# Conformer, attention and experts in one kernel: the normalisation after the convolution by blocks, six taps moved to TensorE

## The chip, the cores and the metric

One core of one Trainium2 chip runs the whole model block. The metric is the device time of one execution in microseconds (us). Before the change it is 1229.51 us, the median of three runs (1229.46 to 1229.88).

## What is computed

The input x is 256 tokens by 1024 channels in float32. Layer 0 is a Conformer convolution module and a dense SwiGLU; layer 1 is attention with forget gates (16 heads) and a SwiGLU of 8 experts of which each token takes 2; an RMSNorm stands before each part and at the end. The change touches the Conformer module alone:

```python
def conformer_conv(h, w_in, b_in, w_dw, b_dw, ln_g, ln_b, w_out, b_out):
    u = h @ w_in + b_in                       # 1024 -> 2048
    a, gate = jnp.split(u, 2, axis=-1)
    u = a * jax.nn.sigmoid(gate)
    u = depthwise_conv(u, w_dw) + b_dw        # 31 taps back in time, each channel by itself
    u = layer_norm(u, ln_g, ln_b)             # over the 1024 channels of a token
    u = jax.nn.silu(u)
    return u @ w_out + b_out
```

## The kernel before, in words

Channels lie in 8 tiles of 128 partitions; the 256 tokens are two blocks of 128, which here are called block 0 and block 1. A float32 matrix product is made of three products of high and low parts (`mm3`): every weight tile of 128x1024 is copied by ScalarE to a high part `wh`, and VectorE subtracts it from the weight to give the low part `wl` (`split`, L93 to L95). One such pair is what the text calls a split. `emit_split` issues the next one; five may stand ready. Weight tiles of 1 MB come by DMA into a ring of 10 slots; when a tile has been used up, `drop` gives its slot to the next tile in a fixed order, and SyncE issues the load, in order, when the slot's last reader is done. `later` is a list of pieces of work that are issued one by one at each use of a weight part, so that other engines' work is put between products.

Every engine does its instructions in the order in which the program issues them. That order is written by hand. In the Conformer module it is:

1. `glu_mm`, `glu_tr`: the products with w_in, the gate (a Sigmoid on ScalarE, L563) and transposes, so that channels lie in partitions.
2. The convolution, by channel tile. Tiles 2, 3, 6 and 7 are products with diagonal weights on TensorE (`conv_pe`, 64 records of 128 columns each). Tiles 0 and 4 are 31 multiply-adds each on VectorE (`conv_dve`). Tile 1 and the first 25 taps of tile 5 are a multiplication on ScalarE into one of four buffers `pr` and an addition on GpSimd each (`conv_pool`, L639 and L640). The last `SHARE` = 6 taps of tile 5 are made on VectorE into `p5` (`shared`, L701), and L720 adds the two parts of tile 5. A list `steps`, sorted by a time written for each step (L711 to L719), sets how these are mixed; the first four splits of w_out stand in it at 17, 20, 23 and 26.
3. The mean over channels: `mean(o)`, a product of each channel tile with a matrix of 1/1024, summed over the 8 tiles in `pm`. Tiles 0 to 3 are issued between the convolution's products, tiles 4, 6, 5 and 7 after the last of them (L722).
4. The variance (L732 to L752): a copy of the mean (`mu`), subtraction of the mean from four halves (VectorE three, GpSimd one), squares on ScalarE, sums over partitions by products with a column `onesd`. The first half's four tiles go to TensorE as they are; the other three halves are first summed over tiles by VectorE (L745). Both blocks' sums lie in one `pq`. A Silu on `mu` makes ScalarE load the table of Silu.
5. `rsqrt` for both blocks at once: small instructions on VectorE, one after another. Then `lrs` is spread over the partitions by a product with the identity into `pb`, and VectorE scales c (`scale_c`, L762), ScalarE applies Silu with gain and bias (L770), VectorE makes high and low parts (L773, L774), block 0 ahead of block 1.
6. The products with w_out (`colmm`, L787): for each half of the columns, block 0 (24 products and one of the bias), then block 1.

`warm(n)` issues n products of 128x128 ones on TensorE whose result nobody reads. Each float32 product shows as two records in the trace. From the dense SwiGLU on, the program is the same before and after.

Of the kernel before, what the change touches and what calls it, by code (L numbers as in the profile page):

```python
# [35 lines left out]
LAG = 2  # L36
SILU = 2
REP = 8
WARM = [16, 9, 2, 8, 8, 7, 8, 5]
HOLD = 2  # L40
SPLITH = 2
WPOOL = 2
# [1 line left out]
DVE_RATE = 0.65  # L44
POOL_RATE = 0.8
SHARE = 6
WHOLE = (5, 15, 25)
PAD = 15
SEG = PAD + P
# [5 lines left out]
def tile_trunk(ctx: ExitStack, tc: tile.TileContext, a):  # L55
# [17 lines left out]
    def mm(o, l, r, start, stop):  # L73
        pe.matmul(o, l, r, start=start, stop=stop)  # L74
# [15 lines left out]
    def f32(t):  # L90
        return t.bitcast(F32)
# [61 lines left out]
    def add(fill, gain=None, width=512, subs=2):  # L153

        tiles.append((fill, gain, width, subs))
        i = len(tiles) - 1
        first[i] = len(order)
        order.extend((i, j) for j in range(subs))
        return i

    def load(t, src):
        src = src() if callable(src) else src
        m = 2 if st["load"] == 0 else 1
        for k in range(m):
            c = slice(k * SLOT // m, (k + 1) * SLOT // m)
            nc.sync.dma_start(t[:, c], src[:, c])
# [5 lines left out]
    def cols(w, gain=None, n=512):  # L172

        m = SLOT // n
        return [add(lambda t, x=next(w): load(t, x), gain and (gain, k), n, 2) for k in range(0, DO, m)][0]
# [32 lines left out]
        free.append(slot_of.pop(i))  # L208
        push()

    def emit_split():
        n = st["split"]
        i, j = order[n]
        _, gain, width, subs = tiles[i]
        src = slot_of[i][:, 1024 * j:1024 * j + 1024]
        if gain == "whole":
            parts[n] = (src,)
            st["split"] += 1
            return
        hi = cst.tile([P, 1024], F32R, name="wh", tag="wh", bufs=NSPLIT)  # L220
        lo = cst.tile([P, 1024], F32R, name="wl", tag="wl", bufs=NSPLIT)
        if gain is None:
            split(hi, lo, src, g if st.get("pool") and n % st["pool"] == 0 else v)
        else:
            for q in range(1024 // width):
                k = gain[1] + j * (1024 // width) + q
                c = slice(q * width, q * width + width)
                x = gain[0][:, k:k + 1]
                s.activation(hi[:, c], src[:, c], AF.Copy, scale=x)  # L229
                v.scalar_tensor_tensor(lo[:, c], src[:, c], x, f32(hi[:, c]), ALU.mult, ALU.subtract)  # L230
        parts[n] = (hi, lo)
        st["split"] += 1
        if j == subs - 1:
            drop(i)

    def split_ahead():
# [35 lines left out]
    w = stream(a["dense"])  # L272
    L_in = [cols(w) for _ in range(4)]
    L_diag = [add(lambda t, x=next(w): load(t, x), subs=0) for _ in range(8)]
    L_wout = [cols(w) for _ in range(2)]
    L_ffn = add_ffn(w, vcol("ffn", 0))
    gk = vcol("kv")
# [15 lines left out]
    L_moe = [add_moe(i, WHOLE if i % 2 else ()) for i in range(E)]  # L293


    def rsqrt(dst, var, mul=1.0, add=0.0):

        n = var.shape[-1]
        hv, y, q = (tmp.tile([P, 2], F32, name=x, tag=x, bufs=1)[:, :n] for x in ("hv", "y", "q"))
        sh = tmp.tile([P, 2], I32, name="sh", tag="sh", bufs=1)[:, :n]  # L300
        v.tensor_scalar(hv, var, 0.5 * mul, 0.5 * add, ALU.mult, ALU.add)
        v.tensor_scalar(sh, hv.bitcast(I32), 1, None, ALU.arith_shift_right)
        v.tensor_scalar(y.bitcast(I32), sh, -1.0, float(0x5F3759DF - 2 ** 22 - 2 ** 31), ALU.mult, ALU.add)
        for it in range(3):
            for b in range(n):
                c = slice(b, b + 1)
                v.scalar_tensor_tensor(q[:, c], y[:, c], hv[:, c], y[:, c], ALU.mult, ALU.mult)
            v.scalar_tensor_tensor(dst if it == 2 else y, q, 1.5, y, ALU.subtract, ALU.mult)

    def sum_squares():  # L310
        ms = tmp.tile([P, 2], F32, name="ms", tag="ms", bufs=1)
# [159 lines left out]
    with convs:  # L471
# [57 lines left out]
        warm(WARM[5])  # L529
        lay(0)  # L530
        lay(1)

# [158 lines left out]
        p5 = phases(bank("dn")[:, :NT])  # L691

        def mean(o):
            mm(pm, onesq, cT[:, o], o == 0, o == DO - 1)

        def shared(j):
            w = wdwT[:, 5, j:j + 1]
            if j == CW - SHARE:
# [6 lines left out]
        def at_time(t, dt, fs):  # L705
            for f in fs:
                steps.append((t, len(steps), f))
                t += dt
            return t

        t = at_time(1.5, 0.42, qd + taps_of(conv_dve, 4))  # L711
        at_time(t, 0.42, [lambda j=j: shared(j) for j in range(CW - SHARE, CW)])
        at_time(1.5, 0.8, qp + taps_of(conv_pool, 5)[:CW - SHARE])
        at_time(7.8, 0, [out2])
        at_time(14.8, 0, [out3] + [lambda o=o: mean(o) for o in range(4)])
        at_time(21.8, 0, [out6])
        at_time(17, 3, [emit_split] * 4)
        for _, _, f in sorted(steps):
            f()  # L719
        v.tensor_tensor(c5, c5, p5, ALU.add)  # L720
        conv_pe(7)()
        for o in (4, 6, 5, 7):  # L722
            mean(o)
        warm(WARM[1])


# [2 lines left out]
        sq = [xp[:, t].rearrange("p (o c) -> p o c", c=P) for t in range(2)]  # L729
        halves = (slice(0, 4), slice(4, 8))  # L730
        mu = cv.tile([P, 2, HP], F32, name="mu")
        s.activation(mu, pmb[1], AF.Copy)  # L732
        pq = bank("dn")
        for t in range(2):
            for x in halves:
                c = cb[t][:, x]
                on_pool = t == 1 and x is halves[0]
                (g if on_pool else v).tensor_tensor(
                    c, c, (mu if on_pool else pmb[t])[:, None].to_broadcast([P, 4, 2, HP]), ALU.subtract)
                s.activation(sq[t][:, x].rearrange("p o (b m) -> p o b m", b=2), c, AF.Square)  # L740
        for o in range(4):
            mm(pq[:, 0:1], sq[0][:, o], onesd, o == 0, False)
        for t, x in ((0, halves[1]), (1, halves[0]), (1, halves[1])):
            sr = cv.tile([P, P], F32, name="sr", tag="sr", bufs=2)
            v.tensor_reduce(sr, sq[t][:, x].rearrange("p o c -> p c o"), AX.X, ALU.add)  # L745
            warm(WARM[2])
            mm(pq[:, t:t + 1], sr, onesd, False, t == 1 and x is halves[1])
        s.activation(mu, mu, AF.Silu)
        lrs = cv.tile([P, 2], F32, name="lrs")
        lv = cv.tile([P, 2], F32, name="lv")  # L750
        v.tensor_scalar(lv, pq[:, :2], EPS, None, ALU.add)
        rsqrt(lrs, lv)  # L752
        warm(WARM[3])
        pb = bank("dn")
        for t in range(2):
            mm(pb[:, P * t:P * t + P], lrs[:, t:t + 1].to_broadcast([P, P]), ident, t == 0, t == 1)

        warm(WARM[4])

        def scale_c(t, x):  # L760
            r = pb[:, P * t:P * t + P].rearrange("p (b m) -> p b m", b=2)[:, None]
            v.tensor_tensor(cb[t][:, x], cb[t][:, x], r.to_broadcast([P, x.stop - x.start, 2, HP]), ALU.mult)  # L762

        scale_c(0, slice(0, 2))
        scale_c(0, slice(2, 8))
        for t in range(2):
            h, l = [y[:, :, P * t:P * t + P].rearrange("p o (m b) -> p o b m", b=2) for y in hT]
            for o in range(DO):
                c = cb[t][:, o]
                s.activation(c, c, AF.Silu, scale=vcol("lng")[:, o:o + 1], bias=vcol("lnb")[:, o:o + 1])  # L770
                if o % 2 or t == 0 and o == 0:
                    x = slice(o - 1 if o > 1 or t else o, o + 1)
                    v.tensor_copy(h[:, x], cb[t][:, x])  # L773
                    v.tensor_tensor(l[:, x], cb[t][:, x], f32(h[:, x]), ALU.subtract)  # L774
                if t == 0 and o in (3, 5):
                    scale_c(1, halves[o // 2 - 1])

        for hf in range(2):
            ps = [bank() for _ in range(2)]
# [20 lines left out]
    with tc.tile_pool(name="att", bufs=1, reuse_waits="tile") as ap:  # L800
# [272 lines left out]
        rms_inv(R2)  # L1073
        logit(1, 0)
        logit(1, 1)
        warm(WARM[6])
        high(0, 1)
        high(1, 0)
        lg = ap.tile([P, 2, E], F32, name="lg")
# [14 lines left out]
        warm(WARM[7])  # L1094
# [310 lines left out]
def _laid_out(i):  # L1405
# [26 lines left out]
    for q in range(8):  # L1432

        ch = P * (4 * (q // 4) + 2 + q % 4 // 2) + HP * (q % 2) + c
        for b in range(2):
            diag[q, HP * b + c, 1 - b:32 - b, c] = dw[:, ch].T
    w_in, w_out, kvf, wq = i["conv_w_in"][0], i["conv_w_out"][0], i["w_kvf"], i["w_q"][0]
    dense = [cols(w_in, c0) for c0 in (0, 1024, 512, 1536)] + [diag.reshape(8, P, SLOT)]
# [55 lines left out]
```

## Time and profile before

| | |
|---|---|
| time, median of 3 runs | 1229.51 us (1229.46 to 1229.88) |
| profiled execution, its own time | 1228.05 us |
| its span, first to last instruction | 1226.3 us |
| mean granted clock of TensorE | 0.992 |
| busy share: PE, DVE, ACT, POOL | 96%, 80%, 70%, 8% |
| DMA | 356.17 MB, mean 290 GB/s |

PE is TensorE's matrix products, PEld its weight loads, DVE VectorE, ACT ScalarE, POOL GpSimd, SP SyncE. Times in the rows are in us from the start of the span. A row of a timeline merges neighbouring instructions of one kind: its first number is the start of the first, its second the time that they cover or take, and x the count. In square brackets stands the time that the engine had been idle, and what it had waited for.

### The profile page before, as it was taken

The numbers are of one execution on the slowest core, as the hardware profiler recorded it, in microseconds if no ns is written. First come the engines' busy times: TensorE is split into PE (matmuls) and PEld (weight loads), VectorE is DVE, ScalarE is ACT, GpSimd is POOL, SyncE is SP. The second block draws the span as 40 slices with busy tenths as digits, with TensorE's granted clock in tenths as the row PEclk, the third lists the DMA queues.
The fourth block names the chain that finished last, engine by engine and source line by source line (L and its number), as shares of the span: only waits on it lengthen the run. The fifth ranks groups of instructions, "written<-read, shape, count | busy, mean of one in ns | idle before, by whom it ended". The sixth has DMA issues, their size and how long they took to land.

```text
span 1226.3 us, 17350 instructions
## 1 busy us (share of the span) xinstructions
PE 1180.0 (96%) x6036; PEld 958.9 (78%) x6036; DVE 980.1 (80%) x1343; ACT 854.0 (70%) x1194; POOL 94.1 (8%) x114
## 2 busy tenths in 40 slices
PE   8997999999999989999999999999999999999995
PEld 6796888888889758788778888778888778888774
DVE  5787755645667548998899999899999899999886
ACT  5785654545566557777778778778778778778785
POOL 0483000000001560000000000000000000000000
PEclk9998999999999999999999999999999999999998
DMA  9963445545544336898899999999999999999961
GB/s 359 376 207 138 181 164 206 176 172 202 175 167 145 136 117 245 313 379 319 351 420 376 374 365 358 366 420 386 372 363 354 369 419 388 370 364 359 364 253 55
DMA packets 50625, 356.17 MB, mean 290 GB/s; under 512 B 5857, under 2 KB 6113, under 8 KB 8033
## 3 DMA queue, kind: packets, MB, share of 16 engines
q1 hardware_dynamic: 49808, 354.23, 75.5%
q8 instruction: 49, 0.80, 0.3%
q10 hardware_dynamic: 720, 0.75, 0.2%
q14 instruction: 48, 0.39, 0.1%
HBM read 353.91 MB, written 1.05 MB: 289 GB/s over the span
## 4 chain that ended last, share of the span: by engine, by line
PE 85%; DVE 6%; ACT 3%; issue 3%; POOL 2%; DMA 1%; SPq 0%; ACTq 0%; DVEq 0%; POOLq 0%
PE mm L74 55%; PE dn L74 19%; PE tp L74 8%; DVE wl L95 3%; POOL cT L640 2%; ACT wh L94 1%; DMA ring<-in_dense_dram 1%; PE tp L415 1%; DVE xres L371 1%; DVE sa L911 1%; DVE sm L910 1%; PE mm L415 0%; PE tp L925 0%; POOL pb L919 0%; ACT ysh L1322 0%
## 5 line engine op out<-in xcount | busy, mean ns | idle before, releaser
L95 DVE TENSOR_TENSOR wl<-ring,wh 128x1024 fp32r<-128x1024 f32 x440 | 523.0, 1226 | 84.3 <-ACT wh L94 80.5
L94 ACT ACTIVATE wh<-ring 128x1024 fp32r<-128x1024 f32 x446 | 456.1, 1055 | 95.5 <-PE mm L74 69.0
L230 DVE SCALAR_TENSOR_TENSOR wl<-ring,vec,wh 128x512 fp32r<-128x512 f32 (+1 forms) x144 | 95.9, 718 | 66.1 <-ACT wh L229 66.0
L74 PE MATMUL mm<-wh,xgh 128*128 128x512 f32 (+1 forms) x384 | 146.8, 382 | 0.0
L74 PE MATMUL mm<-wl,xgh 128*128 128x512 f32 (+1 forms) x384 | 144.3, 376 | 1.7 <-DVE wl L95 1.7
L74 PE MATMUL mm<-wh,xgl 128*128 128x512 f32 (+1 forms) x384 | 144.6, 377 | 0.4 <-ACT xgl L1229 0.4
L95 DVE TENSOR_TENSOR wl<-more,wh 128x1024 fp32r<-128x1024 f32 x112 | 133.3, 1221 | 11.6 <-ACT wh L94 10.5
L229 ACT ACTIVATE wh<-ring,vec 128x512 fp32r<-128x512 f32 (+1 forms) x144 | 91.5, 690 | 69.4 <-PE mm L74 45.3
L74 PE MATMUL mm<-wh,hTh 128*128 128x512 f32 (+1 forms) x344 | 135.6, 394 | 3.1 <-ACT wh L94 1.9
L74 PE MATMUL mm<-wh,xg 128*128 128x512 f32 (+1 forms) x352 | 134.9, 390 | 0.0
L74 PE MATMUL mm<-wl,hTh 128*128 128x512 f32 (+1 forms) x344 | 132.4, 385 | 1.6 <-DVE wl L95 1.6
L74 PE MATMUL mm<-wl,xg 128*128 128x512 f32 (+1 forms) x352 | 132.9, 385 | 0.0
L74 PE MATMUL mm<-wh,hTl 128*128 128x512 f32 (+1 forms) x344 | 132.3, 384 | 0.0
L94 ACT ACTIVATE wh<-more 128x1024 fp32r<-128x1024 f32 x112 | 115.4, 1057 | 15.2 <-PE mm L74 7.1
L74 PE MATMUL dn<-wh,acth 128*128 128x512 f32 x220 | 86.5, 393 | 0.0
L74 PE MATMUL dn<-wh,actl 128*128 128x512 f32 x220 | 86.2, 392 | 0.0
L74 PE MATMUL dn<-wl,acth 128*128 128x512 f32 x220 | 86.2, 392 | 0.0
L74 PEld LDWEIGHTS mm<-wl,xgh 128*128 128x128 f32 x384 | 72.1, 188 | 16.8 <-DVE wl L95 2.2
L74 PEld LDWEIGHTS mm<-wl,xg 128*128 128x128 f32 x352 | 66.4, 189 | 23.2 <-DVE wl L95 11.1
L74 PEld LDWEIGHTS mm<-wh,xgl 128*128 128x128 f32 x384 | 72.3, 188 | 14.4 <-ACT xgl L1229 0.7
L74 PEld LDWEIGHTS mm<-wh,xgh 128*128 128x128 f32 x384 | 72.2, 188 | 13.7
L74 PEld LDWEIGHTS mm<-wh,hTh 128*128 128x128 f32 x344 | 64.6, 188 | 18.6 <-ACT wh L94 2.5
(314 smaller groups left out, 1852.3 us busy)
## 6 DMA issues: line engine op xcount, KB each, us to landing
ring<-in_routed_dram SPq DMA_DIRECT2D x204, 1024.0 KB, 7.3
ring<-in_dense_dram SPq DMA_DIRECT2D x68, 1024.0 KB, 4.9
more<-in_routed_dram SPq DMA_DIRECT2D x60, 1024.0 KB, 7.4
xT<-in_xT_dram SPq DMA_DIRECT2D x2, 512.0 KB, 6.8
ring<-in_dense_dram SPq DMA_DIRECT2D x2, 512.0 KB, 7.4
xp<-in_x_dram SPq DMA_DIRECT2D x2, 512.0 KB, 13.6
xres<-in_x_dram SPq DMA_DIRECT2D x1, 1024.0 KB, 16.5
kT<-in_rows_dram SPq DMA_DIRECT2D x1, 512.0 KB, 5.7
```

The source lines that it names most:

```text
L74: pe.matmul(o, l, r, start=start, stop=stop)
L94: s.activation(hi, src, AF.Copy)
L95: (lo_eng or v).tensor_tensor(lo, src, f32(hi), ALU.subtract)
L229: s.activation(hi[:, c], src[:, c], AF.Copy, scale=x)
L230: v.scalar_tensor_tensor(lo[:, c], src[:, c], x, f32(hi[:, c]), ALU.mult, ALU.subtract)
L371: v.tensor_tensor(x, x, ps, ALU.add)
L415: pe.transpose(pt[:, P * j:P * j + P], ac[:, P * j:P * j + P], ident)
L640: g.tensor_tensor(c, c, pr, ALU.add)
L910: v.scalar_tensor_tensor(sm[:, x], ps[:, x], Fq[:, b, h:h + 1], mask[:, x], ALU.add, ALU.add)
L911: v.tensor_reduce(sa[:, b:b + 1], sm[:, x], AX.X, ALU.max, negate=True)
```

## The change

It has these parts.

- a. A Sigmoid on a column of ones at the program's start, on ScalarE.
- b. `LAST` = 6: the last six taps of channel tile 5 become six products with diagonal weights of 128x128 on TensorE (`last_taps`), issued after `conv_pe(7)`. Their weights (393 KB) are one more load in the ring, between the convolution's and w_out's. GpSimd and ScalarE make 19 taps of tile 5 in place of 25, VectorE the six after them. VectorE adds the products' result to c5.
- c. The four splits leave the list of steps. Two come after L720's addition; two come after `conv_pe(7)`, and of these VectorE's part is put off: one stands after the addition of `last_taps`, one after the subtraction of the mean.
- d. Means in the order 4, 6, 7, then 5.
- e. The variance by blocks: VectorE's three sums over tiles and the addition of EPS are gone, each block's eight tiles of squares are summed by products with the column, in a `pq` of its own, block 0 ahead of block 1. Block 0: 8 column products, `warm(9)`, `rsqrt`, the spreading product. Then block 1's 8 column products and `warm(3)`.
- f. The nine small instructions of block 1's `rsqrt` are put in pairs between the instructions that make block 0's high and low parts. The spreading product, scaling, Silu and parts of block 1 go into `later`, from the fifth use of w_out's parts on, which is in block 0's products.

```diff
-WARM = [16, 9, 2, 8, 8, 7, 8, 5]
+WARM = [16, 9, 9, 3, 7, 8, 5]
...
+LAST = 6
...
+    s.activation(cst.tile([P, 1], F32, name="half"), one, AF.Sigmoid)
...
-    def emit_split():
+    def emit_split(low=None):
...
+        if low is not None:
+            s.activation(hi, src, AF.Copy)
+
+            def late():
+                v.tensor_tensor(lo, src, f32(hi), ALU.subtract)
+                if j == subs - 1:
+                    drop(i)
+
+            low.append(late)
...
     L_diag = [add(lambda t, x=next(w): load(t, x), subs=0) for _ in range(8)]
+    L_last = add(lambda t, x=next(w): nc.sync.dma_start(t[:, :P * LAST], x[:, :P * LAST]), subs=0)
...
+        def last_taps():
+
+            x = phases(bank()[:, :NT])
+            for k in range(LAST):
+                mm(x, slot_of[L_last][:, P * k:P * k + P], tap(5, CW - LAST + k), k == 0, k == LAST - 1)
+            drop(L_last)
+            return x
...
-        at_time(t, 0.42, [lambda j=j: shared(j) for j in range(CW - SHARE, CW)])
-        at_time(1.5, 0.8, qp + taps_of(conv_pool, 5)[:CW - SHARE])
+        at_time(t, 0.42, [lambda j=j: shared(j) for j in range(CW - LAST - SHARE, CW - LAST)])
+        at_time(1.5, 0.8, qp + taps_of(conv_pool, 5)[:CW - LAST - SHARE])
...
-        at_time(17, 3, [emit_split] * 4)
         for _, _, f in sorted(steps):
             f()
         v.tensor_tensor(c5, c5, p5, ALU.add)
+        emit_split()
+        emit_split()
         conv_pe(7)()
-        for o in (4, 6, 5, 7):
+        low = []
+        emit_split(low)
+        emit_split(low)
+        pl5 = last_taps()
+        for o in (4, 6, 7):
             mean(o)
+        v.tensor_tensor(c5, pl5, c5, ALU.add)
+        low[0]()
+        mean(5)
         warm(WARM[1])
...
         for t in range(2):
             for x in halves:
+                center(t, x)
+        low[1]()
+        variance(0, slice(0, DO))
+        warm(WARM[2])
+        run(inverse(0))
         s.activation(mu, mu, AF.Silu)
+        everywhere(0)
+        variance(1, slice(0, DO))
         warm(WARM[3])
+        two = [slice(o, o + 2) for o in range(0, DO, 2)]
+        scale_c(0, two[0])
         scale_c(0, slice(2, 8))
+        aside.extend(inverse(1))
+        for x in (slice(0, 1), slice(1, 2), *two[1:]):
+            silus(0, x)
+        beside(9)
+        later.append([[lambda: None] * 4
+                      + [lambda: (everywhere(1), scale_c(1, two[0]), scale_c(1, slice(2, 8)), silus(1, two[0]))]
+                      + [lambda x=x: silus(1, x) for x in two[1:]], 0, 1])
```

The functions that it calls:

```python
def silus(t, x):
    ...
    for o in range(x.start, x.stop):
        c = cb[t][:, o]
        s.activation(c, c, AF.Silu, scale=vcol("lng")[:, o:o + 1], bias=vcol("lnb")[:, o:o + 1])
    v.tensor_copy(h[:, x], cb[t][:, x])
    beside()        # two of block 1's small instructions, while there are any
    v.tensor_tensor(l[:, x], cb[t][:, x], f32(h[:, x]), ALU.subtract)
    beside()

def variance(t, x):
    for o in range(x.start, x.stop):
        mm(pq[t], sq[t][:, o], onesd, o == 0, o == DO - 1)
```

## Rows read from the trace of the kernel before

**Rows 1.** The page's first part: busy us, share of the span and instructions of each engine.

```profile
PE 1180.0 (96%) x6036; PEld 958.9 (78%) x6036; DVE 980.1 (80%) x1343; ACT 854.0 (70%) x1194; POOL 94.1 (8%) x114
```

**Rows 2.** The chain of waits, the piece of it from 99 to 135 us (start, us, what).

```profile
99.86 0.73 POOL cT L640
...
100.62 0.43 DVE cT L720
...
114.04 20.36 PE mm L74 x87
```

**Rows 3.** TensorE's timeline from the last of the convolution to the products with w_out.

```profile
84.53 1.89 PE L74 MATMUL tp<-cT,onesq 128*128 128x256 f32 x8
86.26 7.31 PE L74 MATMUL mm<-u,ring 128*128 128x128 f32 x64
93.40 1.03 PE L74 MATMUL tp<-cT,onesq 128*128 128x256 f32 x4
101.10 2.08 PE L74 MATMUL tp<-cT,onesq 128*128 128x256 f32 x4 [6.67 <-DVE cT L720]
102.96 2.95 PE L74 MATMUL tp<-one 128*128 128x128 f32 x18
105.75 0.95 PE L74 MATMUL dn<-onesd,xp 128*128 128x1 f32 x8
106.56 0.69 PE L74 MATMUL tp<-one 128*128 128x128 f32 x4
...
108.56 0.38 PE L74 MATMUL dn<-onesd,sr 128*128 128x1 f32 x2
...
111.55 0.71 PE L74 MATMUL dn<-ident,lrs 128*128 128x128 f32 x4 [0.71 <-DVE lrs L308]
112.09 1.95 PE L74 MATMUL tp<-one 128*128 128x128 f32 x16
113.80 0.47 PE L74 MATMUL mm<-wh,hTh 128*128 128x512 f32 x1
...
119.80 0.39 PE L74 MATMUL mm<-wh,hTh 128*128 128x512 f32 x1
```

**Rows 4.** GpSimd's timeline and the durations (min/median/max ns) of its additions.

```profile
68.28 32.30 POOL L640 TENSOR_TENSOR cT<-cT,pr 128x256 f32<-128x256 f32 x36 [3.78 <-ACT pr L639]
...
L640 POOL TENSOR_TENSOR cT<-cT,pr x54: 722/732/1602, 47.4 to 99.9; 128x256 f32<-128x256 f32 x54
```

**Rows 5.** VectorE's timeline: the splits at the convolution's end, the subtraction of the mean, `rsqrt` and the first scaling; then the durations (min/median/max ns) of the high and low parts by tiles of channels (one tile, or two).

```profile
84.37 1.77 DVE L95 TENSOR_TENSOR wl<-ring,wh 128x1024 fp32r<-128x1024 f32 x1
...
90.13 1.73 DVE L95 TENSOR_TENSOR wl<-ring,wh 128x1024 fp32r<-128x1024 f32 x1
...
96.10 3.10 DVE L95 TENSOR_TENSOR wl<-ring,wh 128x1024 fp32r<-128x1024 f32 x2
103.52 1.88 DVE L738 TENSOR_TENSOR cT<-cT,tp 128x512 f32<-128x512 f32 x3 [2.48 <-ACT mu L732]
...
108.98 0.16 DVE L751 TENSOR_SCALAR lv<-dn 128x2 f32<-128x2 f32 x1 [0.47 <-PE dn L74]
...
109.78 0.35 DVE L307 SCALAR_TENSOR_TENSOR q<-y,hv 128x1 f32<-128x1 f32 x2
110.17 0.16 DVE L308 SCALAR_TENSOR_TENSOR y<-q,y 128x2 f32<-128x2 f32 x1
...
112.29 1.29 DVE L762 TENSOR_TENSOR cT<-cT,dn 128x256 f32<-128x256 f32 x2 [0.80 <-PE dn L74]
...
L773 DVE CAST hTh<-cT x9: 220/288/298, 113.5 to 119.7; 128x256 fp32r<-128x256 f32 x7, 128x128 fp32r<-128x128 f32 x2
L774 DVE TENSOR_TENSOR hTl<-cT,hTh x9: 292/426/427, 113.8 to 120.0; 128x256 fp32r<-128x256 f32 x7, 128x128 fp32r<-128x128 f32 x2
```

**Rows 6.** ScalarE's timeline: its first two loads of tables and what stands behind them, the squares, and the Silus.

```profile
6.30 1.28 ACT L486 ACT_TABLE_LOAD   x1 [6.30 <-DMA xT<-in_xT_dram]
8.67 1.06 ACT L94 ACTIVATE wh<-ring 128x1024 fp32r<-128x1024 f32 x1 [0.17 <-DMA ring<-in_dense_dram]
...
35.91 1.28 ACT L563 ACT_TABLE_LOAD   x1
37.20 1.27 ACT L563 ACTIVATE sg<-mm,rs 128x512 f32<-128x512 f32 x2
...
104.24 2.33 ACT L740 ACTIVATE xp<-cT 128x512 f32<-128x512 f32 x4 [0.76 <-DVE cT L738]
...
112.81 6.32 ACT L770 ACTIVATE cT<-cT,vec 128x128 f32<-128x128 f32 x16 [4.62 <-DVE cT L762]
```

**Rows 7.** TensorE's timeline beside the second of these loads.

```profile
36.26 1.08 PE L74 MATMUL mm<-bhl,bl 128*128 128x512 f32 x4
37.94 0.50 PE L74 MATMUL mm<-wh,hTh 128*128 128x512 f32 x1 [0.60 <-ACT sg L563]
```

**Rows 8.** Stretches: the busy time of PE, PEld, DVE, ACT and POOL (with counts), the granted clock of TensorE, the DMA share and GB/s.

```profile
10.00:15.00 5.00, 3.60 (x13) 2.02 (x13) 3.94 (x7) 3.61 (x7) 0.00 (x0) 1.00 1.02 425
...
98.00:100.00 2.00, 0.00 (x0) 0.00 (x0) 1.21 (x1) 0.00 (x0) 1.84 (x3) 0.50 0.00 0
...
110.00:120.00 10.00, 9.29 (x54) 7.85 (x53) 8.74 (x30) 7.19 (x17) 0.00 (x0) 1.00 0.00 0
```

**Rows 9.** Who waited for whom (us in total, times, longest): ScalarE's splits for the ring's loads, in the first 130 us.

```profile
ACT wh L94 <- DMA ring<-in_dense_dram: 1.6, 2, 1.4
```

More of the change, by code (lines that the diff above doesn't have):

```diff
@@ L221, in emit_split @@
         lo = cst.tile([P, 1024], F32R, name="wl", tag="wl", bufs=NSPLIT)
-        if gain is None:
+        if low is not None:
[5 more added lines that the diff above has]
+            low.append(late)
+        elif gain is None:
             split(hi, lo, src, g if st.get("pool") and n % st["pool"] == 0 else v)
@@ L232, in emit_split @@
         st["split"] += 1
-        if j == subs - 1:
+        if j == subs - 1 and low is None:
             drop(i)
@@ L293, in tile_trunk, with rsqrt_steps @@
     L_moe = [add_moe(i, WHOLE if i % 2 else ()) for i in range(E)]
-    def rsqrt(dst, var, mul=1.0, add=0.0):
+    def rsqrt_steps(dst, var, mul=1.0, add=0.0):
         n = var.shape[-1]
@@ L300, in rsqrt @@
         sh = tmp.tile([P, 2], I32, name="sh", tag="sh", bufs=1)[:, :n]
-        v.tensor_scalar(hv, var, 0.5 * mul, 0.5 * add, ALU.mult, ALU.add)
-        v.tensor_scalar(sh, hv.bitcast(I32), 1, None, ALU.arith_shift_right)
-        v.tensor_scalar(y.bitcast(I32), sh, -1.0, float(0x5F3759DF - 2 ** 22 - 2 ** 31), ALU.mult, ALU.add)
+        yield lambda: v.tensor_scalar(hv, var, 0.5 * mul, 0.5 * add, ALU.mult, ALU.add)
+        yield lambda: v.tensor_scalar(sh, hv.bitcast(I32), 1, None, ALU.arith_shift_right)
+        yield lambda: v.tensor_scalar(y.bitcast(I32), sh, -1.0, float(0x5F3759DF - 2 ** 22 - 2 ** 31), ALU.mult, ALU.add)
         for it in range(3):
@@ L306, in rsqrt @@
                 c = slice(b, b + 1)
-                v.scalar_tensor_tensor(q[:, c], y[:, c], hv[:, c], y[:, c], ALU.mult, ALU.mult)
-            v.scalar_tensor_tensor(dst if it == 2 else y, q, 1.5, y, ALU.subtract, ALU.mult)
+                yield lambda c=c: v.scalar_tensor_tensor(q[:, c], y[:, c], hv[:, c], y[:, c], ALU.mult, ALU.mult)
+            yield lambda it=it: v.scalar_tensor_tensor(dst if it == 2 else y, q, 1.5, y, ALU.subtract, ALU.mult)
+    def rsqrt(*x):
+        for f in rsqrt_steps(*x):
+            f()
     def sum_squares():
@@ L528, in tile_trunk @@
         push()
-        warm(WARM[5])
+        warm(WARM[4])
         lay(0)
@@ L693, in mean @@
         def mean(o):
-            mm(pm, onesq, cT[:, o], o == 0, o == DO - 1)
+            mm(pm, onesq, cT[:, o], o == 0, o == 5)
+        def last_taps():
[4 more added lines that the diff above has]
+            return x
         def shared(j):
             w = wdwT[:, 5, j:j + 1]
-            if j == CW - SHARE:
+            if j == CW - LAST - SHARE:
                 v.tensor_scalar(p5, tap(5, j), w, None, ALU.mult)
@@ L731, in tile_trunk, with center @@
         mu = cv.tile([P, 2, HP], F32, name="mu")
+        lrs = cv.tile([P, 2], F32, name="lrs")
         s.activation(mu, pmb[1], AF.Copy)
-        pq = bank("dn")
+        pb = {}
+        def center(t, x):
+            c = cb[t][:, x]
+            on_pool = t == 1 and x is halves[0]
+            (g if on_pool else v).tensor_tensor(
+                c, c, (mu if on_pool else pmb[t])[:, None].to_broadcast([P, 4, 2, HP]), ALU.subtract)
+            s.activation(sq[t][:, x].rearrange("p o (b m) -> p o b m", b=2), c, AF.Square)
@@ new lines, in tile_trunk, with inverse, everywhere, scale_c @@
+        pq = [bank("dn")[:, :1] for _ in range(2)]
+        def variance(t, x):
+            for o in range(x.start, x.stop):
+                mm(pq[t], sq[t][:, o], onesd, o == 0, o == DO - 1)
+        def inverse(t):
+            return rsqrt_steps(lrs[:, t:t + 1], pq[t], 1.0, EPS)
+        def everywhere(t):
+            x = bank()[:, :P]
+            mm(x, lrs[:, t:t + 1].to_broadcast([P, P]), ident, True, True)
+            pb[t] = x.rearrange("p (b m) -> p b m", b=2)[:, None]
+        def scale_c(t, x):
+            v.tensor_tensor(cb[t][:, x], cb[t][:, x], pb[t].to_broadcast([P, x.stop - x.start, 2, HP]), ALU.mult)
@@ new lines, in tile_trunk, with beside @@
+        aside = []
+        def beside(n=2):
+            run(aside[:n])
+            del aside[:n]
+        def silus(t, x):
+            h, l = [y[:, :, P * t:P * t + P].rearrange("p o (m b) -> p o b m", b=2) for y in hT]
+            for o in range(x.start, x.stop):
+                c = cb[t][:, o]
+                s.activation(c, c, AF.Silu, scale=vcol("lng")[:, o:o + 1], bias=vcol("lnb")[:, o:o + 1])
+            v.tensor_copy(h[:, x], cb[t][:, x])
+            beside()
+            v.tensor_tensor(l[:, x], cb[t][:, x], f32(h[:, x]), ALU.subtract)
+            beside()
@@ L734, in tile_trunk @@
         for t in range(2):
             for x in halves:
[L736 to L747, printed above, removed]
+                center(t, x)
@@ L748, in tile_trunk @@
+        low[1]()
+        variance(0, slice(0, DO))
+        warm(WARM[2])
+        run(inverse(0))
         s.activation(mu, mu, AF.Silu)
[L749 to L752, printed above, removed]
+        everywhere(0)
+        variance(1, slice(0, DO))
         warm(WARM[3])
-        pb = bank("dn")
-        for t in range(2):
-            mm(pb[:, P * t:P * t + P], lrs[:, t:t + 1].to_broadcast([P, P]), ident, t == 0, t == 1)
@@ L758, in tile_trunk @@
[L758 to L764, printed above, removed]
-        scale_c(0, slice(2, 8))
[L766 to L776, printed above, removed]
+        two = [slice(o, o + 2) for o in range(0, DO, 2)]
@@ L1075, in tile_trunk @@
         logit(1, 1)
-        warm(WARM[6])
+        warm(WARM[5])
         high(0, 1)
@@ L1093, in tile_trunk @@
         mm(ps[:, E:2 * E], oner.to_broadcast([P, P]), M[:, 0], False, True)
-        warm(WARM[7])
+        warm(WARM[6])
         gained(1, 1, v)
@@ L1436, in _laid_out @@
             diag[q, HP * b + c, 1 - b:32 - b, c] = dw[:, ch].T
+    last = np.zeros((1, P, 16, P), np.float32)
+    c = np.arange(P)
+    for k in range(LAST):
+        last[0, c, k, c] = dw[CW - LAST + k, 5 * P + c]
     w_in, w_out, kvf, wq = i["conv_w_in"][0], i["conv_w_out"][0], i["w_kvf"], i["w_q"][0]
-    dense = [cols(w_in, c0) for c0 in (0, 1024, 512, 1536)] + [diag.reshape(8, P, SLOT)]
+    dense = [cols(w_in, c0) for c0 in (0, 1024, 512, 1536)] + [diag.reshape(8, P, SLOT), last.reshape(1, P, SLOT)]
     dense += [cols(w_out, c0) for c0 in (0, 512)]
```

## The prediction

> **What bounds the kernel now.** I read the page's first part, then the chain of waits, then each engine's timeline round the change, then the stretches. TensorE is busy for 96% of the span [rows 1]. In the chain the stage in question is the exception: at 99 to 101 us it runs through GpSimd and VectorE, then through small steps, and from 114.04 it is an unbroken run of 87 products [rows 2]. TensorE's timeline shows why: the convolution's last product tile and two means are issued by 94.4; then it waits 6.67 us for the addition that completes channel tile 5 [rows 3], which waits for GpSimd's last of 36 additions, at 100.6 [rows 2, 4]. While it waits its clock falls to half (0.50 at 98 to 100) [rows 8]. Block 0's first product with w_out starts at 113.80, block 1's at 119.80 [rows 3]. I compute the new time of that last event. From there the products are the same, the ring is full (no DMA traffic at 110 to 120 [rows 8]), and what starts earlier should end as much earlier.
>
> **a. The Sigmoid at the start: 0.** It runs before 6.30, where ScalarE waits for its first data, and the table of Sigmoid is then present. Two loads of 1.28 us go. The one at 6.30 hides already: the first split waits until 8.67 for the ring's load, 0.17 us after ScalarE was free [rows 6]. The one at 35.91 ends at 37.19, the Sigmoid starts at 37.20 [rows 6]; but what it reads comes from the third of four bias products started at 36.26, so at about 37.1 [rows 7]. Gain 0.1 at least, 1.28 at most were the products not there; I take 0, as the products are.
>
> The Trainium skill ("ScalarE: Activation LUTs", section "What ACT_TABLE_LOAD costs") counts 2.66 us for each switch, a load of 1283 ns and a drain of 1380 ns. The rows agree on the load and show the next activation 0.01 us behind it, so no drain. By the page the sum would be up to 2.6 us larger.
>
> **b and c. The end of the convolution.** GpSimd's 36 additions took 32.3 us; four of them, beside VectorE's four splits, took about 1.6 in place of 0.73 [rows 4]. So the pitch without these is (32.3 - 4 x 0.87)/36 = 0.80, and 30 additions end at 68.28 + 24.0 = 92.3. VectorE's last tap ended at 96.10 with two splits before it, 1.77 and 1.73 long [rows 5]; without them, less 0.1 of overlap, at 92.7. L720's addition (0.43) then ends at 93.2, two splits (3.1 for two beside GpSimd [rows 5]; without it less, I take 1.23 each) at 95.6.
>
> TensorE comes to the six new products at 93.40 [rows 3]. Products of this kind are not in the trace, but the means have their shape: 8 records in 1.73 us, 0.216 each; at half clock 4 in 1.86, 0.465 [rows 3]. Twelve records cost 2.6 (bounds 2.6 and 5.6); I take 2.6, as nothing idles before them. At 96.0 three means follow (1.3), to 97.3. VectorE, free since 95.6, adds the new part at 96.2 to 96.6, so mean 5 finds it ready and is issued by 97.7. The split put off (1.23) ends at 97.8, where VectorE needs the mean only at 98.2: it costs nothing, and up to 1.2 if the addition came late. ScalarE's four high parts have the room that six multiplications and four splits left.
>
> The new load of 393 KB takes a ring slot, so every later load comes one release later, and SyncE's queue now holds the convolution's last slots back behind the splits, to 95.6 (for the last split to about 101). That is covered by the 10 us without traffic before 120 [rows 8], and ScalarE's splits wait but 1.6 us for the ring in the first 130 [rows 9]. Cost 0; without that cover it would be one tile of 1 MB at the 425 GB/s of rows 8, 2.5 us.
>
> **d and e. Mean and variance.** The last mean's result is there at 97.9; the subtraction followed 0.34 behind it (103.18 to 103.52 [rows 3, 5]), so 98.2, and the squares 0.72 behind that, 0.57 each [rows 6]: block 0's are ready at 99.5 and 100.1. TensorE meanwhile does `warm(9)`, 18 records at 0.107 (16 in 1.71 at full clock [rows 3]), to 99.65, then 16 column records at 0.101 (8 in 0.81 [rows 3]), to 101.3. The squares are in time, so TensorE's order is the bound here. VectorE reads 0.3 after the last issue (108.56 + 0.1 to 108.98 [rows 3, 5]), at 101.6. Nine small instructions: three at 0.20 and three pairs at 0.40 (for one column, half of q's 0.35 and y [rows 5]), 1.8, to 103.4. `warm(9)` ends at 103.2, so the spreading product goes at 103.45. Before, VectorE started 0.74 after it with four records (111.55 to 112.29 [rows 3, 5]); with two, 0.53: at 104.0. The three sums over tiles and the EPS step are simply gone from VectorE.
>
> TensorE goes on: 2 + 16 records to 105.3, `warm(3)` to 105.95. That is when its first product can go; it was 113.80.
>
> **f. Block 0's parts with block 1's steps between them.** VectorE scales for 1.29 [rows 5], to 105.25; the first Silu (0.4 to 0.5) fits beside the second part. The first high part ends at 105.5. Now block 1's first small instruction waits for its column sums, readable at 105.6; queued behind it on VectorE stand all low parts, and TensorE waits for those. Pairs of 0.4 between parts of 0.25 and 0.3 (one tile) or 0.30 and 0.43 (two) [rows 5]: low part 0 at 106.3, high 1 at 106.95, low 1 at 107.65, high 2 and 3 at 108.35, low at 109.0. So TensorE does 7 products from 105.95 to 109.05, where 25 took 6.00 before (0.24 each [rows 3]): 1.4 us of new stall. From the eighth on parts run ahead: 18 products (one of bias) and the spreading product, 4.5, and block 1 can start at 113.6. Bounds for the stall: 0, if the pairs fit between products, and 1.8 + 0.4, if every small instruction is waited for.
>
> Block 1 then: VectorE ends block 0's parts at 110.4, the fifth split at 111.6, scaling of two tiles 112.05, two Silus 112.95, high and low parts 113.7; its second product is due at 113.84. Just in time, and the next ones have more room.
>
> **Sum.** Block 1 starts at 113.6 in place of 119.80: 6.2 us less. Span 1220.1, that execution's own time 1228.05 - 6.2 = 1221.85. The median shown, 1229.51, stands 1.46 above that execution; I keep this and predict 1223.3.
>
> **Rivals.**
> 1. The feed of GpSimd stays the limit. If the 18 additions of tile 5 end only with ScalarE's outputs between them, say at 97 as they would with splits where they were and six additions fewer (100.6 - 4.8, and one slot lost), L720 ends at 97.4, the two splits ahead of the second addition 99.9, mean 5 starts at 100.4, 3.1 late: gain 3.1, 1226.4. For it: VectorE's splits now stand ahead of the addition. Against: the pitch of 0.80 is GpSimd's own work, 0.73 and the gap.
> 2. The table's load does come out of the path, 1.2 us more: 1222.1. For: the Sigmoid starts right behind it. Against: the bias products.
> 3. Slower: the clock. From 99.65 TensorE has column products, warming products and, in block 0, waits between products. If the clock falls there and stays at half until block 1, the 12.2 us of issue (6.0 of records, 6.2 of block 0) take 12.2 more, of which 1.6 vanish in waits: block 1 starts at 124.2, 4.4 later than before, 1233.9. It outweighs the gain from 7.8 us of issue at half clock on. One spell like that of the trace, 6.7 us (97.8 to 104.5), costs 3.4: 1226.7. Against: at 10 to 15 us TensorE was busy for 3.60 of 5 with waits between products, and had 1.00 [rows 8]; column products and warming products in turns follow at 105.75 [rows 3] without a fall.
>
> The Trainium skill ("TensorE: Matmul & The Clock Gate", section "A second HAM failure mode: psum-queue depth-cycling") speaks against the change here: short idle times between groups of products made the clock swing between half and full. The 1.00 at 10 to 15 us does not bear it out for gaps of this size; by the page the result would be rival 3's.
>
> 4. The change does not do what it says: block 1's steps end late and block 1 stalls for what block 0 won. A stall of 3 us would leave 1226.3; the working above has it just in time, so I count it with rival 1.
>
> **Chances.** Forecast 0.66 (its own range 1222.0 to 1225.0), rivals 1 and 4 0.12, rival 2 0.06, one spell of half clock 0.09, the clock at half throughout 0.05, nothing gained for another reason 0.02. The range 1221.5 to 1226.9 leaves out the last two, a tenth of the forecast and part of the spell. 0.2% is 2.46 us, about what a measurement of this kernel can tell: faster means under 1227.05. Faster 0.86, within 0.08, slower 0.06.
>
> **What would show it.** Right: no wait of TensorE over 1 us between the last convolution tile and w_out; clock 1.00 from 90 to 120; GpSimd's last addition near 92; block 0's first product near 106, its first seven taking 3 us, block 1's first near 113.6; the Sigmoid at 37.1. Wrong: a wait of mean 5 for L720's successor (rival 1), a clock of 0.50 after 99 (rival 3), TensorE waiting at block 1's first tiles (rival 4), or a later stage that waits for DMA.

## The result

The kernel after takes 1223.86 us (median of 7 runs, 1221.34 to 1225.89), the kernel before beside it 1229.51: a ratio of 0.995, interval 0.9939 to 0.9961. By the medians that is 5.65 us less, by the ratio's interval 4.8 to 7.5; forecast were 6.2 and 1223.3, the range was 1221.5 to 1226.9. The profiled execution took 1223.72, its span is 1221.9.

TensorE's timeline of the kernel after, over the stretch of [rows 3]:

```profile
92.73 2.76 PE L75 MATMUL mm<-uT,ring 128*128 128x256 f32 x12
95.32 1.89 PE L75 MATMUL tp<-cT,onesq 128*128 128x256 f32 x8
97.05 2.17 PE L75 MATMUL tp<-one 128*128 128x128 f32 x18
99.06 1.85 PE L75 MATMUL dn<-onesd,xp 128*128 128x1 f32 x16
100.77 2.25 PE L75 MATMUL tp<-one 128*128 128x128 f32 x18
102.88 0.49 PE L75 MATMUL mm<-ident,lrs 128*128 128x128 f32 x2
103.21 1.84 PE L75 MATMUL dn<-onesd,xp 128*128 128x1 f32 x16
104.91 0.91 PE L75 MATMUL tp<-one 128*128 128x128 f32 x6
105.58 0.48 PE L75 MATMUL mm<-wh,hTh 128*128 128x512 f32 x1
...
107.67 0.50 PE L75 MATMUL mm<-wh,hTl 128*128 128x512 f32 x1
...
112.20 0.39 PE L75 MATMUL mm<-wh,hTh 128*128 128x512 f32 x1
```

No row has a bracket: the wait of 6.67 us is gone and none took its place. From the end of the convolution's last tile to block 1's first product with w_out (called the interval from here on) it is 112.20 - 92.73 = 19.47 us; before it was 119.80 - 93.40 = 26.40 [rows 3]. So the stage won 6.93. The 0.67 by which this execution stands ahead at 92.73 does not come from this stage: it is 0.74 at the first product with data already (9.04 after, 9.78 before), and in the runs below whose program is the same up to the normalisation this point lies at 92.56 to 93.68.

The clock in these stretches (PE, PEld, DVE, ACT, POOL busy, granted clock, DMA share, GB/s):

```profile
98.00:100.00 2.00, 2.00 (x21) 2.00 (x20) 2.00 (x4) 1.70 (x4) 0.87 (x1) 1.00 1.00 418
...
106.00:108.00 2.00, 2.00 (x8) 1.06 (x7) 1.90 (x11) 2.00 (x5) 0.00 (x0) 1.00 1.03 426
```

It is 1.00 (2.4 GHz) where it was 0.50 (1.2 GHz) [rows 8]. GpSimd, VectorE and ScalarE after, in this order, each answering to a step of the prediction:

```profile
67.61 24.06 POOL L658 TENSOR_TENSOR cT<-cT,pr 128x256 f32<-128x256 f32 x30 [3.73 <-ACT pr L657]
```

```profile
92.55 0.42 DVE L745 TENSOR_TENSOR cT<-cT,dn 128x256 f32<-128x256 f32 x1
92.89 2.35 DVE L96 TENSOR_TENSOR wl<-ring,wh 128x1024 fp32r<-128x1024 f32 x2
95.52 0.42 DVE L755 TENSOR_TENSOR cT<-mm,cT 128x256 f32<-128x256 f32 x1 [0.27 <-PE mm L75]
...
100.94 0.16 DVE L315 TENSOR_SCALAR hv<-dn 128x1 f32<-128x1 f32 x1 [0.37 <-PE dn L75]
...
105.09 0.16 DVE L315 TENSOR_SCALAR hv<-dn 128x1 f32<-128x1 f32 x1 [0.19 <-PE dn L75]
105.28 0.15 DVE L316 TENSOR_SCALAR sh<-hv 128x1 int32<-128x1 int32 x1
105.35 0.28 DVE L808 TENSOR_TENSOR hTl<-cT,hTh 128x128 fp32r<-128x128 f32 x1
...
107.53 0.29 DVE L806 CAST hTh<-cT 128x256 fp32r<-128x256 f32 x1
```

```profile
36.52 1.27 ACT L581 ACTIVATE sg<-mm,rs 128x512 f32<-128x512 f32 x2 [1.27 <-PE mm L75]
```

The stage won 6.93, yet the whole execution only 4.4 of span. Where the rest went is read from the start of the same instruction at later places. First the kernel before (the transposed forget logits, a copy ahead of the experts, the last multiplication; first and last start stand behind the durations):

```profile
L839 ACT ACTIVATE zT<-tp x1: 356/356/356, 345.4 to 345.4; 16x256 f32<-16x256 f32 x1
...
L1132 DVE COPY G<-R x1: 172/172/172, 479.5 to 479.5; 128x16 f32<-128x16 f32 x1
...
L1207 DVE CAST ST<-tp x8: 414/416/419, 483.4 to 997.5; 128x256 fp32r<-128x256 f32 x8
...
L1368 DVE TENSOR_TENSOR yo<-xres,fg x2: 683/684/684, 1214.1 to 1214.7; 128x512 f32<-128x512 f32 x2
```

Then the kernel after:

```profile
L894 ACT ACTIVATE zT<-tp x1: 354/354/354, 338.0 to 338.0; 16x256 f32<-16x256 f32 x1
...
L1187 DVE COPY G<-R x1: 168/168/168, 473.2 to 473.2; 128x16 f32<-128x16 f32 x1
...
L1262 DVE CAST ST<-tp x8: 412/416/420, 477.1 to 991.3; 128x256 fp32r<-128x256 f32 x8
...
L1423 DVE TENSOR_TENSOR yo<-xres,fg x2: 684/685/686, 1209.3 to 1209.9; 128x512 f32<-128x512 f32 x2
```

The lead is 7.60 at block 1's products (0.67 of it from the start), 7.4 at 338, 6.3 at 473, 6.2 at 991 and 4.8 at 1209. So in this pair of executions most of it goes in two places, 1.1 in the attention and 1.4 between 991 and 1209. The granted clock of the kernel after shows what lies there:

```profile
424.00:446.00 22.00, 18.27 (x98) 12.41 (x97) 9.71 (x25) 10.14 (x27) 13.68 (x14) 0.92 0.24 90
...
754.00:774.00 20.00, 18.04 (x78) 13.04 (x78) 16.78 (x19) 13.61 (x19) 0.00 (x0) 1.00 0.91 342
1122.00:1136.00 14.00, 12.11 (x46) 9.35 (x45) 11.52 (x13) 8.43 (x12) 0.00 (x0) 0.88 0.92 343
```

and the one of the kernel before in the same stretches:

```profile
424.00:446.00 22.00, 18.23 (x108) 12.19 (x106) 11.15 (x34) 11.44 (x33) 11.36 (x13) 1.00 0.32 120
...
1122.00:1136.00 14.00, 12.12 (x53) 9.59 (x52) 12.94 (x13) 11.46 (x13) 0.00 (x0) 1.00 0.98 367
```

A spell of half clock at 440 us and one at 1130 us stand in this profile of the kernel after and not in that of the kernel before; one at about 580 both have (0.91 after and 0.96 before over 566 to 584, before partly behind it). The one at 1130 begins behind a wait of TensorE of 1.89 us for VectorE, of which the experts' scatters have four, and three of 0.7 to 0.9; the kernel before has the same waits.

That the kernel after as such loses this, the pair does not show. The profiled execution of the kernel before (1228.05 us, mean clock 0.992) is faster than each of the seven runs timed beside the kernel after (1229.31 to 1231.56), while the 1223.72 of the kernel after lies beside its median. The profile of e1, which is the kernel before with one Sigmoid more, has a spell at 1130 as well (0.83 over 1130 to 1140), and that of e3, whose time is within 0.1% of the kernel before, has one in the attention (0.83 over 440 to 450). And the 6.93 lies inside the 4.8 to 7.5 us of the ratio.

### The profile page after: what moved, and what is told of

It reads as the page before. It is cut to its first block, busy times and chain, and to the rows that moved or that the text cites. A ratio compares the mean times of both kernels' runs of the same rounds, so it can differ in the third digit from the quotient of the medians.

```text
span 1221.9 us, 17357 instructions
## 1 busy us (share of the span) xinstructions
PE 1183.8 (97%) x6046; PEld 962.4 (79%) x6046; DVE 976.9 (80%) x1346; ACT 850.9 (70%) x1188; POOL 86.0 (7%) x108
## 4 chain that ended last, share of the span: by engine, by line
PE 89%; DVE 5%; issue 2%; ACT 2%; DMA 1%; SPq 0%; DVEq 0%; ACTq 0%
PE mm L75 59%; PE dn L75 20%; PE tp L75 8%; DVE wl L96 2%; ACT wh L95 1%; DMA ring<-in_dense_dram 1%; PE tp L433 1%; DVE xres L389 1%; DVE sa L966 1%; DVE sm L965 1%; PE mm L433 0%; PE tp L980 0%; ACT junk L341 0%; ACT pb L967 0%; ACT ysh L1377 0%
```

## The experiments

Each was timed beside the kernel before on the same chip. "Interval" is the one defined above, from the profile.

**e1_sigmoid_only: part a alone.**

```diff
+    s.activation(cst.tile([P, 1], F32, name="half"), one, AF.Sigmoid)
```

> The kernel before with part a alone (the Sigmoid at the start). Theory of the prediction: both loads of tables that go had been hidden, so nothing to gain; the interval of the ratio holds 1.000, and from the last bias product (36.3 us before) to the next product (37.9 us) stays 1.6 us. Rival: the load at 35.9 us was on the path, 1.2 us earlier from there on, about 1228.3 us.

Measured: ratio 1.0002 (0.9992 to 1.0013); from the bias products at 36.25 to the next product at 37.89 it is 1.64 us, before 1.68 [rows 7]. By the interval the gain is 1.0 us at most, so both loads had been hidden, and the rival with its 1.2 us falls.

**e2_tail_only and e3_blocks_only: the change in two halves.** e2 has parts a to d and the old normalisation, with `low[1]()` behind the subtraction; e3 has the old convolution and parts e and f.

```diff
# e2, against the kernel after
-        variance(0, slice(0, DO))
-        warm(WARM[2])
-        run(inverse(0))
+        for o in range(4):
+            mm(pq[:, 0:1], sq[0][:, o], onesd, o == 0, False)
+        for t, x in ((0, halves[1]), (1, halves[0]), (1, halves[1])):
+            sr = cv.tile([P, P], F32, name="sr", tag="sr", bufs=2)
+            v.tensor_reduce(sr, sq[t][:, x].rearrange("p o c -> p c o"), AX.X, ALU.add)
+            warm(2)
...
# e3, against the kernel after
-        pl5 = last_taps()
+        at_time(17, 3, [emit_split] * 4)
...
```

> The kernel after with parts a to d, but the normalisation as it was before (both blocks at once, VectorE's sums over tiles). From the end of the convolution's last tile to block 1's first product with w_out it took 26.4 us before and 19.5 after. Theory 1 (most of the gain is the wait for channel tile 5): the mean is there 5.3 us earlier, of which 1.2 go to the split that now stands ahead of the sums over tiles, so 22.3 us, and no stretch of half clock between 90 and 120. Theory 2 (most of the gain is the normalisation by blocks): 25 us or more.

> The kernel before with parts e and f alone (normalisation by blocks), its convolution and its splits as before. Theory 1: the wait of 6.7 us and the half clock stay, and the blocks bring 0 to 1 us: 25.4 to 26.4 us from the last tile to block 1's first product, and a time within 0.2% of before. Theory 2: the blocks bring 3 us or more: 23 us.

Measured: e2 0.9973 (0.9963 to 0.9983), e3 0.9991 (0.9981 to 1.0001). Of e2's TensorE:

```profile
93.14 2.76 PE L75 MATMUL mm<-uT,ring 128*128 128x256 f32 x12
...
101.97 0.38 PE L75 MATMUL dn<-onesd,sr 128*128 128x1 f32 x2 [0.99 <-DVE sr L780]
...
104.07 3.44 PE L75 MATMUL tp<-one 128*128 128x128 f32 x16
107.30 0.87 PE L75 MATMUL dn<-ident,lrs 128*128 128x128 f32 x4
...
115.73 0.39 PE L75 MATMUL mm<-wh,hTh 128*128 128x512 f32 x1
```

Of e3's:

```profile
93.71 1.03 PE L74 MATMUL tp<-cT,onesq 128*128 128x256 f32 x4
...
119.19 0.39 PE L74 MATMUL mm<-wh,hTh 128*128 128x512 f32 x1
```

The interval of e2 is 22.59 (won 3.8), e3's 119.19 - 93.71 = 25.48 (won 0.9). Theory 1 stands: the tail (parts a to d) is the larger part, the blocks alone bring under 1 us. But the halves add up to 4.7 and together bring 6.93: once the tail is mended, the blocks are worth 3.1 (22.59 - 19.47), of which the split that e2 puts ahead of the sums over tiles takes a part (expected: 1.2). e2 shows another reason: with the old normalisation TensorE waits 0.99 us for a sum over tiles, and the clock, which theory 1 expected at 1.00, falls: 16 warming records took 3.23 us at 104.07 where they took 1.71 before [rows 3].

**e4_no_warm and e11_no_warm_behind_sums: the warming products.** e4 leaves all three groups out, e11 only the nine behind block 0's sums.

```diff
-WARM = [16, 9, 9, 3, 7, 8, 5]
+WARM = [16, 0, 0, 0, 7, 8, 5]      # e4
+WARM = [16, 9, 0, 3, 7, 8, 5]      # e11
```

> The kernel after without the three groups of warming products in the normalisation (9, 9 and 3 products). Theory W (they hold the clock up): TensorE then has waits of 2 us between 97 and 105 us, the granted clock falls to 0.50 there or in block 0's products, and block 1 starts at least 1 us later than the 19.5 us. Theory N (not needed): the clock stays 1.00, the column products start when the squares are there, and block 1 starts 0.3 to 0.5 us earlier.

> The kernel after without the nine warming products behind block 0's sums, the other two groups kept. Theory C (column products do not hold the clock): TensorE then has one group of 9 between 97 and 99, columns, a wait of 2 us, columns, and 3; the clock falls to 0.50 between 103 and 108 and block 1 starts 1 to 2 us later (20.5 to 21.5 us). Theory N: column products count as work, a wait of 2 us alone does nothing, 19.5 us.

Measured: e4 0.9972 (0.9961 to 0.9982), interval 117.31 - 93.36 = 23.95; e11 0.9967 (0.9958 to 0.9977), interval 115.01 - 92.81 = 22.20. First and last row of e4's interval with its stretches, then the last row of e11's with its own:

```profile
93.36 2.76 PE L75 MATMUL mm<-uT,ring 128*128 128x256 f32 x12
...
117.31 0.39 PE L75 MATMUL mm<-wh,hTh 128*128 128x512 f32 x1
```

```profile
101.00:111.00 10.00, 7.94 (x32) 7.15 (x32) 5.07 (x26) 6.06 (x12) 0.00 (x0) 0.50 0.90 378
111.00:113.00 2.00, 2.00 (x6) 1.55 (x5) 1.93 (x8) 0.00 (x0) 0.00 (x0) 0.50 0.03 8
```

```profile
115.01 0.39 PE L75 MATMUL mm<-wh,hTh 128*128 128x512 f32 x1
```

```profile
97.00:103.00 6.00, 3.99 (x36) 3.88 (x34) 4.78 (x14) 4.17 (x7) 1.27 (x1) 1.00 0.96 404
...
104.00:110.00 6.00, 6.00 (x24) 5.42 (x24) 4.96 (x22) 4.23 (x9) 0.00 (x0) 0.53 0.90 374
```

Theory W stands. What theory C expected came too, at a higher price, 2.7 us; its cause is not shown by it, as e11 has, beside the column products, a wait of 2.06 us that the kernel after does not have. In e4 TensorE was busy for 7.94 of 10 us with column products and block 0's products, and the clock was still 0.50. So the 21 products whose result nobody reads are worth 4.5 us of interval (the kernel before had 31 in this place). This is the mechanism of the prediction's rival 3, and what kept it from coming.

**e9_no_taps: without part b.** 25 taps on GpSimd and six on VectorE as before; two splits ahead of L720's addition.

```diff
-        at_time(1.5, 0.8, qp + taps_of(conv_pool, 5)[:CW - LAST - SHARE])
+        at_time(1.5, 0.8, qp + taps_of(conv_pool, 5)[:CW - SHARE])
...
-        pl5 = last_taps()
...
-        v.tensor_tensor(c5, pl5, c5, ALU.add)
```

> The kernel after without part b: the last six taps stay on VectorE and 25 of tile 5 on GpSimd, two splits stand ahead of L720's addition, two are put off as after; the normalisation is by blocks. Prediction's working for the time without the new products: GpSimd ends at 67.6 + 36 x 0.80 + 2 x 0.87, so 5.6 us behind the last tile's end in place of before it, TensorE waits about 4 us for mean 5 and the clock falls: 21.3 us from the last tile to block 1's first product if the clock holds, 23 if it falls. Rival (the moved splits alone remove the wait, the new products only fill it): 19.5 to 20 us.

Measured: 0.997 (0.9959 to 0.9981), interval 116.45 - 93.12 = 23.33:

```profile
93.12 1.03 PE L75 MATMUL tp<-cT,onesq 128*128 128x256 f32 x4
97.64 0.70 PE L75 MATMUL tp<-cT,onesq 128*128 128x256 f32 x2 [3.49 <-ACT cT L678]
99.15 1.22 PE L75 MATMUL tp<-cT,onesq 128*128 128x256 f32 x2 [0.81 <-DVE cT L746]
100.16 3.33 PE L75 MATMUL tp<-one 128*128 128x128 f32 x18
```

The wait came in the size worked out, 4.3 us in two pieces, and the clock fell (0.55 over 99 to 101). Part b is worth 3.9 us: six products (2.6 us of TensorE) take away the wait and the fall. The first piece was for ScalarE, whose outputs of `conv_pe(7)` stand behind GpSimd's multiplications, which the working had not named.

**e8_not_put_off: the splits' low parts at once.**

```diff
-        emit_split(low)
-        emit_split(low)
+        emit_split()
+        emit_split()
...
-        low[0]()
...
-        low[1]()
```

> The kernel after with VectorE's part of the third and fourth split issued at once, ahead of the addition of the last six taps. Prediction's working: the addition then comes behind 2.4 us of splits that wait for ScalarE's high parts (95.4 and 96.4), so the mean is 1.2 us later: 20.7 us from the convolution's last tile to block 1's first product, and a wait of TensorE of 1 us before mean 5. Rival: the warming products and block 1's room take this up, 19.5 us.

Measured: 0.9957 (0.9944 to 0.997), interval 113.79 - 92.57 = 21.22, 1.75 more than after:

```profile
98.11 0.70 PE L75 MATMUL tp<-cT,onesq 128*128 128x256 f32 x2 [1.50 <-DVE cT L755]
```

Mean 5 waits for the addition. The working had the place and the sign; the size that it gave was 1.2.

**e7_steps_later: block 1's steps from the third tile on.**

```diff
-        aside.extend(inverse(1))
         for x in (slice(0, 1), slice(1, 2), *two[1:]):
+            if x.start == 2:
+                aside.extend(inverse(1))
             silus(0, x)
```

> The kernel after with block 1's nine small instructions from the parts of tiles 2 and 3 on, not from tile 0 on. Block 0's 24 products and its bias took 6.6 us after, 6.0 before. Theory P (the prediction: low parts wait behind these steps): 6.0 to 6.2 us, so block 1 starts 0.4 to 0.6 us earlier (19.0 us from the convolution's last tile). Theory Q: the steps come too late for block 1, which then waits what block 0 gained, 19.5 us or more.

Measured: 0.994 (0.9928 to 0.9952); block 0's products from 106.48 to 112.67, 6.19 us, and an interval of 19.04. Theory P stands: low parts did wait behind these steps, and the cost of it is 0.4 us. Against the kernel after the time itself can't tell so little.

**e5_fill and e6_after_again: where the rest of the gain went.** e6 is the kernel after once more. e5 fills the scatters' waits:

```diff
         def scatter(hf, b):
+            if e < E - 1 and (hf, b) == (1, 0):
+                x = bank()
+                for _ in range(3 if e % 2 else 7):
+                    mm(x[:, :P], ones, ones, True, True)
             p_ = bank("mm" if e == E - 1 else "tp")
```

> The kernel after with warming products (7 or 3) ahead of the third product of each expert's scatter, where TensorE waits 1.9 or 0.7 us for VectorE, seven times between 570 and 1130 us; the wait itself stays. Theory S (part of the gain is given back in spells of half clock that such waits bring about): no stretch below 1.00 between 560 and 1190 us, a mean clock of 0.993 or more, and 1 to 3 us less than the kernel after on the same chip. Theory L (the gain is lost to latencies of later stages): the same time and the same spread as the kernel after.

> The kernel after once more, for its spread beside the others. Theory S: from run to run the time goes with the mean clock, some 1.2 us for each 0.0014 of it (3.4 us at half clock in 1222), and the interval from the convolution's last tile to block 1's first product stays 19.5 us within 0.2 in the profile. Theory L: the spread has nothing to do with the clock.

Measured: e5 1221.9 us, 0.9934 (0.9921 to 0.9947); e6 1223.37, 0.9944 (0.993 to 0.9959), interval 112.00 - 92.56 = 19.44. Stretches of e5, then of e6:

```profile
754.00:774.00 20.00, 19.61 (x92) 14.78 (x91) 16.75 (x19) 13.58 (x19) 0.00 (x0) 1.00 0.84 312
1122.00:1136.00 14.00, 13.61 (x64) 10.51 (x63) 12.53 (x14) 9.65 (x13) 0.00 (x0) 1.00 0.90 344
```

```profile
754.00:774.00 20.00, 18.12 (x73) 13.29 (x72) 16.16 (x18) 12.39 (x16) 0.00 (x0) 0.91 0.87 317
1122.00:1136.00 14.00, 12.04 (x51) 9.13 (x50) 11.78 (x14) 9.64 (x13) 0.00 (x0) 1.00 0.95 352
```

e6 is the same program as the kernel after, and its spells lie elsewhere: one at 754 to 774 in place of 1122 to 1136 (over 566 to 584 both have 0.91, e5 1.00). So a spell at a scatter is a matter of the execution, not of the change. With the waits filled none is left at these places in the profile. Over e6's six runs the time goes with the mean clock, from 1219.39 at 0.996 to 1223.86 at 0.991, 0.9 us for each 0.001, hence an estimate of 1.3 for a spell of 0.0014. So far theory S stands: spells set the time from run to run. That filling the waits gains time is only likely: e5 stands 1.5 us under e6, but the two intervals overlap, and e5's six runs spread over the same clocks, 0.991 to 0.996.

That part of the gain is given back by such spells is not borne out. On this chip the mean clock is 0.9897 over the eleven runs of the kernel before and 0.9927 over e6's six, 0.0030 more; the 6.7 us at half clock that the stage itself no longer has are 0.0027 of a span of 1226.3. So the other stages together run at no lower clock after than before, as far as these few runs can tell.

**e10_fill_and_later: e5 and e7 in one.**

> e5_fill and e7_steps_later in one. Theory S and P: 19.0 us from the convolution's last tile to block 1's first product, no stretch under 1.00 between 560 and 1190 us, and a median 1.5 to 2.5 us under that of the kernel after (0.9925 to 0.9935 of before). Rival: the two don't add, 0.994.

Measured: 1221.0 us, 0.9926 (0.9911 to 0.9942), interval 112.02 - 92.98 = 19.04, and 1.00 in the three stretches of e5. It has the lowest ratio of all that ran; that it beats the kernel after (0.995, 0.9939 to 0.9961) is likely by the medians and not shown by the intervals, which overlap by a hair.

## Why the prediction was right

Compared by durations, as the whole stage begins 0.67 earlier in the profile after.

- **a.** Taken as 0, measured as 0 (e1). The reason holds too: the Sigmoid now waits 1.27 us for the bias products. The Trainium skill ("ScalarE: Activation LUTs", section "What ACT_TABLE_LOAD costs") has a drain behind each load, by which, as an estimate, the sum would have been up to 2.6 us larger; e1's ratio shows no such gain.
- **b, c.** GpSimd's 30 additions took 24.06, forecast 24.0. The six products took 95.32 - 92.73 = 2.59, forecast 2.6, at full clock. L720's addition and two splits were done (95.24) when the products ended, and the second addition waited only for the products, 0.27. The extra load cost nothing, as forecast: ScalarE waits for the ring 2.6 us in the whole execution, all of it in the first 20. e9 and e8 give the price of the six products and of the low parts put off: 3.9 and 1.75.
- **d, e.** Warming 2.01 and 2.11 (forecast 1.93 each), columns 1.71 (1.62), the nine steps from 100.94 to 102.88, 1.9 (1.8). From the last tile to block 0's first product 12.85, forecast 12.55.
- **f.** This is the term that was mis-sized. Forecast were 7.65 us from block 0's first product to block 1's; it took 6.62. Against the 6.00 of before that is 0.6 more in place of 1.65, and some 0.2 of either is the spreading product, so the new stall is about 0.4, not 1.4; e7, whose steps come later, has 6.19. I had added block 1's small instructions to the parts at 0.4 a pair, as they stand when each waits for the one before [rows 5]. Put between independent instructions they overlap: nine steps and five parts took 105.09 to 107.53, 2.4 us, where I had counted 3.4; even their durations in the trace add up to 3.1. The bounds, 0 and 2.2, held it.
- **"What starts earlier should end as much earlier".** Within what the times can tell this held. The stage won 6.93, 0.7 more than forecast: 1.0 from f, less 0.3 from d and e. The median fell by 5.65, but the interval, 4.8 to 7.5, holds 6.93; e6, the same program, has by its ratio 6.9 less. In each of the nine runs whose waits in the later stages were left as they are (e2, e3, e4, e6 to e9, e11 and the kernel after) the won interval lies inside the interval of its ratio: 3.8 us of interval and 0.9973 in e2, 5.2 and 0.9957 in e8, 7.4 and 0.994 in e7. What the median lacks of 6.93 is thus of the size of one or two spells and not shown to be a loss. I had weighed the clock only in the stage that changes, while spells elsewhere move a single execution by more than my error. That the median came within 0.6 of the forecast is in part luck: the stage won more than I had worked out, and the median shows less of it.
- **Rivals.** 1 did not come (GpSimd's pitch is its own work). 2 fell with e1. 3 did not come, but its mechanism is real: e4 and e11 make it happen by taking the warming products out. My first witness against it, the clock of 1.00 at 10 to 15 us [rows 8], was one execution: in e4, whose program is the same there, it is 0.66 over 10 to 15. 4 did not come: block 1's products follow each other at 0.23.

Open: the attention's spell at about 440 us. It is missing in the profiles of the kernel before and e1 and stands in all the others, e3 with its old convolution and e5 and e10 among them; its waits were not filled, and what brings it about is not shown. Nor was it told apart whether in e11 the column products or the wait of 2 us between them lets the clock fall; a wait of 1.9 alone was followed by half clock in some executions (e6 at 762 us) and not in others. The new order of the means (d) was not taken out by itself.

## What to carry to other kernels

Where one late operand stops TensorE, price the clock with the wait: here six products more and 21 that nobody reads took the place of a gap of 6.7 us and the half-speed work behind it, and without either, 4 us of the gain were gone. Small dependent instructions of one block cost little between independent parts of another: here fourteen took 2.4 us whose durations add up to 3.1, so the pitch of the chain is too high a price for them. And when one profile before and one after differ in stages that the change never touched, look first where each execution lies among the runs of its kernel, by time and mean clock: a spell of half clock more or less, at a wait that both have, can look like a loss of the change and be one of the execution.

## What was not expected of the hardware

In e4 the clock stayed at 0.50 from 101 to 113 us though TensorE was busy for 7.94 of the first 10 us of it, with column products and products of 512 columns with waits between. The prediction had taken it from [rows 8] that the clock is 1.00 through work like this. And the same wait of 1.88 us in the same program, ending at 761.2, has 1.00 behind it in one execution and 0.50 (762 to 764) in another (the kernel after and e6).
